# Subtracting the softmax maxima by accumulating DMAs in an encoder block on one core

## The chip, the core and the metric

The kernel runs on one core of a Trainium2 chip. The metric is device time in microseconds for one execution. Before the change three runs took 2291.91, 2293.18 and 2293.73 us; the median is 2293.18 us.

The core's engines run beside each other, each through its own queue of instructions, in order: TensorE (PE, with PEld for its weight loads), VectorE (DVE), ScalarE (ACT), GpSimd (POOL) and SyncE (SP). SP and POOL also issue DMAs; the 16 DMA engines carry them. Engines wait for one another by semaphores.

## The reference, cut to what matters

One layer of a bidirectional encoder on 2048 tokens plus 16 meta tokens: a projection, then grouped attention beside a Fourier mix, an output projection, and an MLP with squared ReLU. The change touches the softmax of attention:

```python
def attend(qb):
    s = jnp.einsum('bkgqd,bksd->bkgqs', qb, kt).astype(jnp.float32) * scale
    p = jax.nn.softmax(s, axis=-1).astype(vt.dtype)
    return jnp.einsum('bkgqs,bksd->bkgqd', p, vt)
```

There are 4 query heads and 2 key heads of 128 features, and all is computed in float32. The kernel splits an operand of a product into a high part and a low part (`hi`, `lo`) and multiplies three times (`mm3`, lines 80 to 82). The split is a cast on ScalarE (line 70) and a subtraction on VectorE (line 71).

## The kernel before

Attention is cut into 16 units, each of 256 tokens and one key head, that is 512 columns of queries (two heads). `attention()` is a generator; the Fourier mix, the output projections and the MLP pull steps of it between their own (`att.upto`), so that a unit lies interleaved with other matmuls. Attention runs from about 345 us, when the maxima of unit 0 are ready, to about 1560 us.

A unit's scores are laid out with keys on partitions and queries along the free axis. `scores(u, i)` makes tile i of 128 keys in one of two PSUM banks (tag `S`, two buffers), ScalarE copies it to SBUF (line 773), and two tiles make a *pair* `S` of 128 x 2 x 512 floats, 512 KB. There are eight pairs per unit, eight buffers for them, and a remainder of 96 rows for the meta tokens. A pair is called by its first tile in the rows below: `S_14_6` is the pair of tiles 6 and 7 of unit 14, the pair with j = 3. VectorE keeps a running maximum `M`.

`stats(u)` makes the maximum over all keys for each query, turns it and spreads it over all partitions; ScalarE copies the result from PSUM into `mb` (128 x 512, line 803). Then `softmax(u, i)` runs, i from 0 to 16. At an even i VectorE subtracts `mb` from a pair (line 832) and ScalarE takes the exponential (line 833), in place or, for the first pair, into the sum `acc`. At an odd i VectorE adds the pair to `acc` (line 839), the pair is split into `ph` and `pl`, and TensorE multiplies it with `v` into `o`. Meanwhile `scores(u + 1, i - 2)` fills the next unit's pairs into the buffers that come free. The first two units multiply unsplit (line 842).

The order on each engine is made by the framework's scheduler: it takes the instructions of the traced program by readiness in its own model of time and by their place in the program, and `issue_after` pins a few. So a change of what an instruction waits for can move rows on every engine.

POOL's queue holds the loads of attention (`q`, line 744; `kt`, line 711; `vt`, line 723), and small operations of the Fourier output (`ysq`, `rs_f`). SP's queue loads the MLP's weights (`wr_up`, `wr_dn`; three buffers of 256 KB).

## Time and profile before

| | |
|---|---|
| median of three runs | 2293.18 us |
| span of the profiled execution | 2291.4 us (the timed runs, without a profile, took 0.5 to 2.3 us more) |
| VectorE's subtractions of `mb` from pairs | 128, of 1.218 us each |
| bytes moved by DMA | 307.23 MB, mean 134 GB/s |
| of these through POOL's queue (q0, software) | 42.16 MB, 6.2% of 16 engines' span |

The page has the busy time of each engine, the costliest groups of instructions with their mean time and what ended the idle time before them, and the DMA queues. Other views are drawn from the same execution: busy time in chosen stretches, who waited for whom, and instructions in order of time. In a row of order of time the first number is the start, the second the time taken, and the bracket the idle time before it and what ended it.

The timed runs stand 0.5 to 2.3 us above the span of the profiled execution, which leaves out what lies around the program.

### The profile page before, as it was taken

To read this page: it belongs to the slowest core of one execution; us is meant where nothing else is said; L and a number is where in the kernel's file an instruction comes from. 1 tells how busy PE (TensorE), PEld (TensorE's weight loads), DVE (VectorE), ACT (ScalarE), POOL (GpSimd) and SP (SyncE) were. 2 spreads that over 40 slices of the span, in tenths; PEclk is the share of its full clock that TensorE was granted. 3 is DMA by queue.
4 is the path that set the end of the run, shared out by engine and by line. 5 is a ranking of instruction groups with operands and counts; after the bars stand their busy time and mean duration, and the time that the engine had idled before them with its cause. 6 is when DMAs were issued, how large, how long until landed. Compare 5 with 4: busy or idle time off the path is not lost.

```text
span 2291.4 us, 30005 instructions
## 1 busy us (share of the span) xinstructions
PE 2278.1 (99%) x10846; PEld 1883.0 (82%) x10846; DVE 1718.7 (75%) x2448; ACT 1280.6 (56%) x2303; POOL 184.0 (8%) x235
## 2 busy tenths in 40 slices
PE   9999999999999999999999999999999999999998
PEld 7888988777888888888888888888888888888887
DVE  6435588999986877986887877885875656697796
ACT  6443356566665655665765775664665545543344
POOL 2212120222000000000000100000000000200000
PEclk9999999999999999999999999999999999999999
DMA  6343252543533222333342453224454444865442
GB/s 213 100 119 102 78 169 79 190 137 120 166 117 108 96 87 79 114 114 106 97 157 87 157 175 104 92 82 170 140 177 158 152 152 156 303 193 165 129 138 83
DMA packets 178069, 307.23 MB, mean 134 GB/s; under 512 B 14960, under 2 KB 63728, under 8 KB 177536
## 3 DMA queue, kind: packets, MB, share of 16 engines
q1 hardware_dynamic: 159136, 262.89, 34.9%
q0 software_dynamic: 18640, 42.16, 6.2%
q8 instruction: 85, 1.39, 0.3%
q14 instruction: 64, 0.52, 0.1%
q10 hardware_dynamic: 144, 0.26, 0.0%
HBM read 225.27 MB, written 79.99 MB: 133 GB/s over the span
## 4 chain that ended last, share of the span: by engine, by line
PE 94%; DVE 3%; DMA 1%; ACT 1%; issue 1%; POOL 0%; SPq 0%; POOLq 0%; DVEq 0%; ACTq 0%
PE pdn L80 5%; PE pdn L82 5%; PE pdn L81 5%; PE pup L80 5%; PE pup L82 5%; PE pup L81 5%; PE s L80 3%; PE s L82 3%; PE s L81 3%; PE ux L80 2%; PE ux L81 2%; PE ux L82 2%; PE dx L80 2%; PE dx L82 2%; PE dx L81 2%; PE o L81 2%
## 5 line engine op out<-in xcount | busy, mean ns | idle before, releaser
L80 PE MATMUL pdn<-wh_dn,ah 128*128 128x512 f32 x512 | 201.5, 394 | 0.2 <-ACT r L1154 0.2
L80 PE MATMUL pup<-mTh,wh_up 128*128 128x512 f32 x512 | 201.5, 394 | 0.0
L81 PE MATMUL pup<-mTl,wh_up 128*128 128x512 f32 x512 | 200.7, 392 | 0.0
L82 PE MATMUL pup<-mTh,wl_up 128*128 128x512 f32 x512 | 200.4, 391 | 0.0
L81 PE MATMUL pdn<-wl_dn,ah 128*128 128x512 f32 x512 | 199.9, 390 | 0.0
L82 PE MATMUL pdn<-wh_dn,al 128*128 128x512 f32 x512 | 198.7, 391 | 0.0
L773 ACT COPY S<-s 128x512 f32<-128x512 f32 x256 | 148.4, 584 | 55.6 <-PE s L82 48.5
L70 ACT CAST wh_up<-wr_up 128x512 fp32r<-128x512 f32 x128 | 79.4, 620 | 164.3 <-PE pup L81 76.5
L832 DVE TENSOR_TENSOR S<-S,mb 128x1024 f32<-128x1024 f32 x128 | 154.8, 1218 | 8.4 <-ACT mb L803 8.2
L71 DVE TENSOR_TENSOR pl<-S,ph 128x512 fp32r<-128x512 f32 x196 | 132.3, 696 | 11.0 <-ACT ph L70 10.7
L833 ACT ACTIVATE S<-S 128x1024 f32<-128x1024 f32 x114 | 120.7, 1060 | 34.7 <-DVE S L832 34.1
L70 ACT CAST wh_dn<-wr_dn 128x512 fp32r<-128x512 f32 x128 | 79.1, 620 | 107.9 <-PE pdn L82 52.6
L71 DVE TENSOR_TENSOR wl_up<-wr_up,wh_up 128x512 fp32r<-128x512 f32 x128 | 87.6, 687 | 68.1 <-ACT wh_up L70 63.3
L839 DVE TENSOR_TENSOR acc<-acc,S 128x1024 f32<-128x1024 f32 x110 | 134.1, 1219 | 1.3 <-ACT S L833 1.1
L71 DVE TENSOR_TENSOR wl_dn<-wr_dn,wh_dn 128x512 fp32r<-128x512 f32 x128 | 87.2, 687 | 60.2 <-ACT wh_dn L70 51.8
L70 ACT CAST ph<-S 128x512 fp32r<-128x512 f32 x196 | 118.7, 620 | 15.9 <-PE o L82 12.5
L70 ACT CAST ah<-a 128x1024 fp32r<-128x1024 f32 x56 | 58.5, 1048 | 118.2 <-issue 60.8
L779 DVE TENSOR_TENSOR M<-M,S 128x1024 f32<-128x1024 f32 x96 | 118.0, 1229 | 6.7 <-ACT S L773 6.0
L80 PEld LDWEIGHTS pdn<-wh_dn,ah 128*128 128x128 f32 x512 | 96.1, 188 | 23.5 <-ACT r L1154 3.6
L80 PE MATMUL s<-q,kt 128*128 128x512 f32 (+1 forms) x272 | 113.0, 415 | 0.1
L82 PEld LDWEIGHTS pdn<-wh_dn,al 128*128 128x128 f32 x512 | 96.2, 188 | 19.9
L82 PEld LDWEIGHTS pup<-mTh,wl_up 128*128 128x128 f32 x512 | 96.2, 188 | 19.4
(345 smaller groups left out, 6413.0 us busy)
## 6 DMA issues: line engine op xcount, KB each, us to landing
wr_up<-in_w_up_dram SPq DMA_DIRECT2D x128, 256.0 KB, 2.8
wr_dn<-in_w_down_dram SPq DMA_DIRECT2D x128, 256.0 KB, 2.6
a<-s_d SPq DMA_DIRECT2D x42, 512.0 KB, 3.6
R<-in_w_up_dram SPq DMA_DIRECT2D x16, 1024.0 KB, 5.2
s_d<-s SPq DMA_DIRECT2D x64, 256.0 KB, 2.2
d<-in_w_down_dram SPq DMA_DIRECT2D x26, 512.0 KB, 5.0
s_d<-c SPq DMA_DIRECT2D x48, 256.0 KB, 2.4
x<-in_x_dram SPq DMA_DIRECT2D x16, 512.0 KB, 4.9
```

Source lines behind the costliest of these rows:

```text
L70: self.high = nc.scalar.copy(hi, src)
L71: self.low = nc.vector.tensor_tensor(lo, src, f32v(hi), op=ALU.subtract)
L80: nc.tensor.matmul(out, a[0], b[0], start=first, stop=False, skip_group_check=chain)
L81: nc.tensor.matmul(out, a[0], b[1], start=False, stop=False, skip_group_check=chain)
L82: nc.tensor.matmul(out, a[1], b[0], start=False, stop=last, skip_group_check=chain)
L773: nc.scalar.copy(S[:, i % 2], ps)
L779: nc.vector.tensor_tensor(M, M, S, op=ALU.max)
L832: nc.vector.tensor_tensor(S, S, mb, op=ALU.subtract)
L833: nc.scalar.activation(p, S, AF.Exp, scale=ISQ)
L839: nc.vector.tensor_tensor(acc, acc, p, op=ALU.add)
```

## The change

For the pairs 1 to 7 of each unit the subtraction is no longer an instruction of VectorE. ScalarE writes `mb` negated. Right after it `stats` traces an addition on VectorE for pair 0, and seven DMAs on POOL's queue which add the negated maxima, read twice for the two halves of a pair, to the pair in SBUF (`accum_op=ALU.add`). The remainder of 96 rows stays on VectorE, as an addition. The exponential of a pair now waits for its DMA.

```diff
@@ -800,7 +800,11 @@
             s = state[u]
             pd = rows_to_cols(over_keys(s["M"], f"m{u}", ALU.max), f"m{u}")
             mb = s["mb"] = ap2.tile([P, 512], F32, name=f"mb_{u}", tag="mb", bufs=1)
-            nc.scalar.copy(mb, pd)
+            nc.scalar.activation(mb, pd, AF.Copy, scale=-1.0)
+            both = mb.rearrange("p (o n) -> p o n", o=1).broadcast_to([P, 2, 512])
+            nc.vector.tensor_tensor(s["S"][0], s["S"][0], both, op=ALU.add)
+            for S in s["S"][1:-1]:
+                nc.gpsimd.dma_start(S, both, accum_op=ALU.add)
 
         def softmax(u, i):
 
@@ -809,7 +813,7 @@
             vt = s["v"]
             if i == NT:
                 S = s["S"][-1][:MR]
-                nc.vector.tensor_tensor(S, S, s["mb"][:MR], op=ALU.subtract)
+                nc.vector.tensor_tensor(S, S, s["mb"][:MR], op=ALU.add)
                 nc.scalar.activation(S, S, AF.Exp, scale=ISQ)
                 hi = ap2.tile([P, 512], R32, name="ph_" + nm, tag="ph", bufs=2)
                 acc = s["acc"]
@@ -828,8 +832,6 @@
             acc = s["acc"]
             p = acc if j == 0 and not s["native"] else S
             if i % 2 == 0:
-                mb = s["mb"].rearrange("p (o n) -> p o n", o=1).broadcast_to([P, 2, 512])
-                nc.vector.tensor_tensor(S, S, mb, op=ALU.subtract)
                 nc.scalar.activation(p, S, AF.Exp, scale=ISQ)
                 return
             v = vt[j // 2]
```

The first place is ScalarE's queue in unit 14, from the copy of the first score tile of unit 15 on. `S_14_k` are unit 14's pairs, `ph_14_5` the casts of the pair `S_14_4`, `s_15_k` score tiles of unit 15 in PSUM, and `wh_up` casts of MLP weights. Before:

```order
L773 COPY S_15_0_14039<-s_15_0_14035 128x512
L70 CAST wh_up_1_4_3_14181<-wr_up_1_4_3_14179 128x512
L70 CAST ph_14_5_0_14132<-S_14_4_13434 128x512
L70 CAST ph_14_5_1_14139<-S_14_4_13434 128x512
L773 COPY S_15_0_14039<-s_15_1_14074 128x512
L70 CAST wh_up_1_4_4_14220<-wr_up_1_4_4_14218 128x512
L833 ACTIVATE S_14_6_13499<-S_14_6_13499 128x1024
L773 COPY S_15_2_14111<-s_15_2_14107 128x512
L70 CAST wh_up_1_4_5_14246<-wr_up_1_4_5_14244 128x512
L833 ACTIVATE S_14_8_13590<-S_14_8_13590 128x1024
L70 CAST ph_14_7_0_14198<-S_14_6_13499 128x512
L773 COPY S_15_2_14111<-s_15_3_14146 128x512
```

And the changed kernel, from the same copy on:

```order
L773 COPY S_15_0_14045<-s_15_0_14041 128x512
L835 ACTIVATE S_14_8_13592<-S_14_8_13592 128x1024
L835 ACTIVATE S_14_10_13656<-S_14_10_13656 128x1024
L835 ACTIVATE S_14_12_13720<-S_14_12_13720 128x1024
L70 CAST ph_14_5_0_14137<-S_14_4_13438 128x512
L70 CAST ph_14_5_1_14144<-S_14_4_13438 128x512
L70 CAST wh_up_1_4_3_14185<-wr_up_1_4_3_14183 128x512
L773 COPY S_15_0_14045<-s_15_1_14080 128x512
L835 ACTIVATE S_14_14_13792<-S_14_14_13792 128x1024
L817 ACTIVATE S_14_16_13873<-S_14_16_13873 96x512
L70 CAST wh_up_1_4_4_14224<-wr_up_1_4_4_14222 128x512
L773 COPY S_15_2_14116<-s_15_2_14112 128x512
```

The exponentials have moved up: three of them now stand ahead of the casts of `S_14_4`, and the last pair's and the remainder's ahead of the copy of `s_15_2`, where before the exponential of `S_14_6` was the last to stand there.

The second place is POOL's queue from the load of unit 15's queries on. Before:

```order
L744 DMA q_15_13999<-q_d7_109 128x2x512
L192 TENSOR_TENSOR rs_a_15522<-ms_a_15520,mhalf_100 128x4
L1097 TENSOR_TENSOR rs_m_3_0_15722<-hsm_3_0_15616,mhalf_100 128x1
L1097 TENSOR_TENSOR rs_m_3_1_15726<-hsm_3_1_15621,mhalf_100 128x1
L1097 TENSOR_TENSOR rs_m_3_2_15730<-hsm_3_2_15626,mhalf_100 128x1
```

And the changed kernel:

```order
L744 DMA q_15_14006<-q_d7_109 128x2x512
L807 DMA S_14_2_13365<-mb_14_13924 128x2x512
L807 DMA S_14_4_13438<-mb_14_13924 128x2x512
L807 DMA S_14_6_13502<-mb_14_13924 128x2x512
L807 DMA S_14_8_13592<-mb_14_13924 128x2x512
L807 DMA S_14_10_13656<-mb_14_13924 128x2x512
L807 DMA S_14_12_13720<-mb_14_13924 128x2x512
L807 DMA S_14_14_13792<-mb_14_13924 128x2x512
L807 DMA S_15_2_14116<-mb_15_14657 128x2x512
```

Each unit's seven additions stand in a row, behind the load of the next unit's queries, and the next unit's seven behind them.

## The prediction

> **What bounds the kernel now.** I read the page's busy times first, then the one row for the stretch in which attention runs (345 to 1530 us), then who TensorE waits for in it.

> ```profile
> span 2291.4 us, 30005 instructions
> PE 2278.1 (99%) x10846; PEld 1883.0 (82%) x10846; DVE 1718.7 (75%) x2448; ACT 1280.6 (56%) x2303; POOL 184.0 (8%) x235
> ...
> 345.00:1530.00 1185.00, 1182.55 (x5453) 960.57 (x5452) 990.78 (x1373) 748.22 (x1296) 87.21 (x109) 1.00 0.37 118
> ...
> PE o L81 <- DVE pl L71: 0.8, 3, 0.4
> PE pmt L1126 <- ACT m L1121: 0.6, 1, 0.6
> PE pm_m L787 <- DVE M L768: 0.4, 1, 0.4
> ```

> The second row is time, then busy time of PE, PEld, DVE, ACT and POOL, the granted clock, the share of the 16 DMA engines, and GB/s. PE is busy 1182.55 of 1185.00 us at clock 1.00. VectorE is busy 990.78 of 1185.00, but what TensorE ever waits for in this stretch is 2.45 us in all, and only 1.2 us of that is put down to VectorE (0.8 for `pl`, 0.4 for `M`). So **whatever VectorE is relieved of, at most 2.45 us (0.1%) can be gained here**. The question is only whether the new way of subtracting makes PE wait.

> **The change part by part.** What goes and what carries on:

> ```profile
> L832 DVE TENSOR_TENSOR S<-S,mb 128x1024 f32<-128x1024 f32 x128 | 154.8, 1218 | 8.4 <-ACT mb L803 8.2
> L833 ACT ACTIVATE S<-S 128x1024 f32<-128x1024 f32 x114 | 120.7, 1060 | 34.7 <-DVE S L832 34.1
> L803 ACT COPY mb<-pd_m x16: 567/587/589, 344.9 to 1507.0; 128x512 f32<-128x512 f32 x16
> ```

> Removed: 112 of the 128 subtractions, 112 x 1.218 = 136 us of VectorE. By the waits above this is worth between 0 and 2.45 us; I take 0, because TensorE's work hides it. Pair 0 and the 96-row remainder stay on VectorE as additions of the same size, 0. The sign change rides on the copy of `mb` (0.587 us, 16 times); I take the same 0.59 us, and twice that would be 16 x 0.59 = 9 us of ACT, hidden under its 437 idle us of this stretch.

> Added: 7 DMAs of 512 KB in each of 16 units. The trace has no DMA that adds, and none from SBUF to SBUF. The nearest rows are POOL's plain loads of the same size, one of which (`kt`, at 355) ran almost alone:

> ```profile
> L711 POOL DMA_DIRECT2D kt<-k_d x20: 713/720/742, 314.0 to 1334.1; - x20
> ...
> q0 software_dynamic: 18640, 42.16, 6.2%
> ...
> q0 software_dynamic: 272, 0.52, 25.6%
> ...
> kt<-k_d POOLq DMA_DIRECT2D x1, 512.0 KB, 4.1
> ```

> The first 6.2% is of the whole span: 0.062 x 2291.4 = 142 us for 42.16 MB, so 1.77 us of all 16 engines for 0.524 MB; the window around the single `kt` gives 25.6% of 8 us, 2.05 us. It landed 4.1 us after its issue. An issue holds POOL 0.72 us: 7 x 0.72 = 5.0 us per unit, so POOL hands them out faster than they run. What the unit sees is a first landing L after `mb`, and then one landing every p; of the `kt`'s 4.1 us some 1.8 are its pass, so L = p + 2.3.

> - Lower end: the adding transfer costs a pass like a plain one, p = 1.8, L = 4.1.
> - Middle: to add, the destination is read besides the source, two reads for a write. Twice the page's figure is **p = 3.6**, L = 5.9.
> - Upper end: two reads, while the loads of other queues take some 0.28 of the engines (they are 0.37 busy in the row above, POOL's own loads among it): 3.6 / 0.72 = 5.0, L = 7.3.

> I take p = 3.6. The single `kt` had its engines nearly to itself, while the loads beside a unit's burst are not nothing, so the middle leans on neither.

> Now the place that pays. Before, an exponential stood in ACT's queue where VectorE had time for its subtraction (34.1 of the 34.7 us ahead of them are waits for it), and unit 14's eight ran from 1427.34 to 1457.72. In the changed order they are drawn together: the exponentials of `S_14_8`, `S_14_10` and `S_14_12` stand ahead of the casts of `S_14_4` (`ph_14_5_0`), and that of `S_14_14`, the seventh addition, ahead of the copy of `s_15_2`. **ACT works in order, so a late landing holds up rows that need no DMA.** When TensorE needs these rows, in unit 14:

> ```profile
> 1425.47 0.59 ACT L803 COPY mb<-pd_m 128x512 f32<-128x512 f32 x1 [1.40 <-PE pd_m L796]
> 1427.34 1.06 ACT L833 ACTIVATE acc<-S 128x1024 f32<-128x1024 f32 x1 [1.29 <-DVE S L832]
> ...
> 1442.89 0.62 ACT L70 CAST wh_up<-wr_up 128x512 fp32r<-128x512 f32 x1 [1.91 <-PE pup L81]
> ...
> 1444.38 0.57 ACT L773 COPY S<-s 128x512 f32<-128x512 f32 x1
> ...
> 1446.32 0.39 PE L80 MATMUL o<-ph,vt 128*128 128x512 f32 x1
> ...
> 1451.08 0.39 PE L80 MATMUL s<-q,kt 128*128 128x512 f32 x1
> ...
> 1457.72 1.07 ACT L833 ACTIVATE S<-S 128x1024 f32<-128x1024 f32 x1
> ...
> L813 ACT ACTIVATE S<-S x16: 612/627/633, 379.3 to 1547.6; 96x512 f32<-96x512 f32 x16
> ```

> `mb` is ready at 1426.06. TensorE takes up the third group of `o` at 1446.32. Ahead of it on ACT stand the exponential of the sixth DMA (1.06) and one cast (0.62 as `wh_up`'s), with an estimated 0.2 for the handing over: the sixth has to land by 1444.4, 18.4 us after `mb`. At 1451.08 TensorE starts `s_15_4`, which needs the PSUM bank of `s_15_2` (there are two), whose copy stands behind the seventh exponential: 1.06 + 0.63 (remainder) + 0.62 (`wh_up`) + 0.57 (copy) = 2.9, so the seventh has to land 22.1 us after `mb`. The DMAs land at L + 5p and L + 6p:

> - p = 1.8: 13.1 and 14.9 us. Nothing waits.
> - p = 3.6: 23.9 and 27.5 us, **5.4 us late**.
> - p = 5.0: 32.3 and 37.3 us, 15.2 us late.

> Where the seventh exponential used to stand, at 1457.72, 31.7 us after `mb`, p = 3.6 would have been in time: the new order sets the price as much as the DMA does.

> Within a unit the delays don't add, since TensorE's later needs shift with the first; across units they do, because TensorE has no idle time to take them up. I counted the seventh landing in all sixteen units from ACT's new order and the old times of `mb` (the first 344.9, the last 1507.0, in the row above): it is needed after 20 to 24 us in ten, after 15 to 17 in three (the first two and the last), after 30 to 33 in three. That averages 22.6, so unit 14 stands for the mean. **16 x 5.4 = 86 us.** At p = 5.0 it is 16 x 15.2 = 243 us, at p = 1.8 about 0.

> The rest I cost at nothing. Loads of weights meet fuller DMA engines, but the old kernel has such a stretch, where the engines were 0.91 busy and PE lost nothing:

> ```profile
> 1320.00:1341.00 21.00, 21.00 (x101) 16.75 (x100) 12.20 (x16) 12.73 (x25) 2.16 (x3) 1.00 0.91 295
> ```

> If that cover failed it would show as waits of ACT for `wr_up` and `wr_dn`. On POOL, the powers for `rs_f` (out_f, units 2 to 4) and the loads of `vt` now stand behind seven issues, 5.0 us; the powers are computed a row block ahead, which hides that, and without it three units would lose up to 3 x 5 = 15 us. The loads of `q` and `kt` stand ahead of the seven as before.

> Sum, against the profiled execution: 2291.4 + 0 + 86 = 2377.4 us of span. The median of the runs stands 1.8 us above that span, so **about 2380 us**, 3.8% slower.

> [...]

> **The rivals.**

> 1. *The queue keeps up, no change.* If an adding DMA moves at up to 2.3 us each (L = 4.6), the seventh lands within 18.4 us of `mb`, ahead of the 22.1. Only the first two units and the last would lose some 2 to 4 us each. Time 2291 to 2300. For it: the plain pass of 1.77 us; its price turns where 2.3 + 7p = 22.1, at p = 2.8. Against it: the destination must be read too. [...]
> 2. *Read, add and write one after the other.* If an addition takes its passes in series and shares the engines, p is 7.5 (three plain passes of 1.8, over 0.72), L = 9.8: the seventh lands 54.8 us after `mb`, 32.7 us late, 16 x 32.7 = 523 us, 2816 us. For it: nothing in this trace shows how an addition is pipelined. Against it: plain loads are.
> 3. *VectorE had been the bound after all, faster.* Its third figure in these rows is 95 to 97 of 100 us:

> ```profile
> 400.00:500.00 100.00, 98.74 (x453) 76.09 (x452) 96.69 (x137) 62.22 (x117) 26.98 (x32) 1.00 0.50 164
> 500.00:600.00 100.00, 99.76 (x458) 79.45 (x457) 95.33 (x138) 61.19 (x112) 20.28 (x26) 1.00 0.49 161
> ```

>    With 136 us less, TensorE's 2.45 us and perhaps as much inside rows that count as busy would go: 2288 us. Against it: the waits above.
> 4. *POOL can't hand the seven out at once* and is held until earlier ones have moved, so that `rs_f` and `vt` come late: the 15 us above on top of the forecast, 2395 us.

> **How the numbers follow.** Forecast (two reads, p between 2.8 and 5.0): 58%. Rival 1: 21%. Rival 2 (anything beyond p = 5.0): 13%. Rival 3: 4%. Rival 4: 4%. A measurement of this kernel can tell about 0.2% (4.6 us) from no change. Rival 1 falls half within 0.2% and half above it, and a small part of the forecast's low end comes out as no change: faster 4%, same 12%, slower 84%. The range goes from the lower bound's time, 2291, to p = 5.0, 2293 + 243 = 2536; some 4% lie below and 14% above.

> **What would show it.** Right: in the changed profile PE loses 60 to 150 us between 345 and the last unit, spread over all units; ACT's exponentials wait for DMA landings, and behind them TensorE waits for `ph`, for copies of `s` and for `wh`; the seven landings of a unit come 3 to 4.5 us apart; VectorE's busy time falls by about 136 us; q0 carries 59 MB more and its share rises by some 17% of the span. Wrong: landings under 2.5 us apart with PE at 1182 of 1185 (rival 1), over 5 us apart (rival 2), or PE waiting for `rs_f` or `wr_up` and not for what stands behind an exponential.

## The result and the profile after

The changed kernel takes **2451.64 us** (median of four runs, 2450.76 to 2453.22) against 2293.40 us for the kernel before, run beside it: a ratio of 1.0692, 95% interval 1.0677 to 1.0707. It is 6.9% slower. The forecast was 2380 us, 3.8% slower, with a range up to 2536. The sign and the range held; 72 us of the loss were missing from the sum.

The page of the changed kernel: busy time of the engines, the software DMA queue q0 with packets, MB and its share of 16 engines, and the costliest group that waits (count, then busy time and mean ns, then its idle time and what ended it).

```profile
span 2449.0 us, 30120 instructions
PE 2330.7 (95%) x10846; PEld 1902.4 (78%) x10846; DVE 1606.8 (66%) x2336; ACT 1278.6 (52%) x2303; POOL 319.9 (13%) x347
...
q0 software_dynamic: 49104, 100.89, 19.9%
...
L835 ACT ACTIVATE S<-S 128x1024 f32<-128x1024 f32 x114 | 120.4, 1058 | 170.8 <-DMA S<-mb 168.2
```

ScalarE's 34 us of waiting ahead of the exponentials have become 170.8, nearly all of it for the additions. VectorE is relieved of 112 us (1718.7 to 1606.8), and TensorE, with the same 10846 matmuls, is busy 52.6 us *longer*. That last figure was in no part of the forecast.

The windows view for the stretch in which attention runs in the changed kernel, the columns as in the prediction (time; busy PE, PEld, DVE, ACT, POOL; granted clock; DMA share; GB/s), and behind it the view of cores for the kernel before and for the changed one:

```profile
345.00:1690.00 1345.00, 1236.69 (x5463) 981.58 (x5462) 885.14 (x1269) 751.22 (x1304) 223.19 (x221) 0.96 0.58 148
```

```profile
core 0: 2291.4 us, clock 0.999
```

```profile
core 0: 2449.0 us, clock 0.979
```

The stretch held 5453 matmuls in 1185 us before and holds 5463 in 1345 us now. TensorE is idle in 1345.00 - 1236.69 = 108.3 us of it, where it was idle in 2.45: **105.9 us of waiting**. It is busy 1236.69 instead of 1182.55, **54.1 us longer**, at a mean clock of 0.96. Two different losses, about two to one.

Who TensorE waits for in that stretch (in total, times, longest):

```profile
PE o L80 <- ACT ph L70: 29.9, 9, 7.2
PE s L80 <- ACT S L773: 13.2, 6, 7.7
PE pup L80 <- DVE h L1182: 13.0, 5, 3.5
PE o L81 <- DVE pl L71: 12.7, 11, 5.5
PE pdn L80 <- DVE h L1182: 8.6, 3, 3.7
PE poa L80 <- DMA at<-o_d: 6.3, 1, 6.3
PE pa L570 <- DVE alo L576: 4.9, 1, 4.9
```

The casts `ph` and the copies of `s` behind late exponentials were forecast; with the 2.8 us that the unsplit units wait for exponentials themselves they make 45.9 of the 105.9 us, and 58.6 with `pl`, which VectorE makes from `ph`. `h` (the MLP's rows, 25 us with its smaller rows), `at` (the attention output read back, 10.6 us) and `alo` (the Fourier part) were not.

Unit 14, the unit that carried the prediction: GpSimd's issues of the seven additions in order of time. Its `mb` starts at 1563.30 and is ready at 1563.90.

```profile
1564.32 3.73 POOL L807 DMA_DIRECT2D S<-mb  x3 [7.45 <-ACT mb L803]
1569.89 1.19 POOL L807 DMA_DIRECT2D S<-mb  x1 [1.84 <-DVE pl L71]
1573.76 1.22 POOL L807 DMA_DIRECT2D S<-mb  x1 [2.68 <-DVE acc L841]
1577.40 1.20 POOL L807 DMA_DIRECT2D S<-mb  x1 [2.42 <-DVE pl L71]
1580.85 1.19 POOL L807 DMA_DIRECT2D S<-mb  x1 [2.24 <-DVE h L1182]
```

Three go out at once; the fourth to the seventh only 3.4 to 3.9 us apart, although GpSimd has nothing else to do. The packets of the trace say why: the additions land at 1569.22, 1573.06, 1576.70, 1580.12, 1583.54, 1587.27 and 1592.07, and each issue from the fourth on comes 0.7 us behind the next landing. The releasers in the brackets are VectorE rows that happened to end then; the landing is what fits every row. So the first addition lands 5.3 us after `mb`, the seventh 28.2 us after it, one every 3.8 us (5.9, 27.5 and 3.6 had been forecast). Over all units the medians are 5.3 and 26.6 us, 3.6 us apart.

What the stall in this unit does to the clock, in the windows view of the changed kernel, columns as above:

```profile
1577.00:1585.40 8.40, 7.52 (x33) 5.83 (x32) 4.86 (x7) 4.18 (x5) 2.39 (x2) 1.00 1.10 205
1585.40:1589.30 3.90, 0.43 (x3) 0.01 (x1) 0.03 (x1) 1.63 (x3) 0.00 (x0) 1.00 1.09 255
1589.30:1590.60 1.30, 1.07 (x4) 0.66 (x4) 1.30 (x3) 1.30 (x3) 0.00 (x0) 0.99 1.03 326
1590.60:1594.00 3.40, 3.40 (x10) 2.62 (x8) 2.92 (x3) 1.69 (x4) 0.00 (x0) 0.50 0.79 276
1594.00:1600.00 6.00, 6.00 (x27) 4.69 (x25) 5.37 (x7) 4.41 (x10) 0.00 (x0) 1.00 0.24 76
```

TensorE is idle for 3.5 us up to 1589.3. It resumes at full clock, and then for 3.4 us the clock is 0.50: the matmuls take 0.63 us instead of 0.39 and start 0.43 us apart instead of 0.23. This stall of 3.5 us so cost another 1.7. In the whole of attention the trace's record of the granted clock has 16 such stretches, of 3.41, 6.83 or 10.24 us, 99.0 us in all. Eight of them begin while TensorE still stands, and in 23.9 of the 99.0 us it does nothing that half speed could slow; the other 75.1 us cost it 37.5 us. Of the 54.1 us that it is busy longer, another 2.2 are the ten matmuls more that the stretch holds; of the remaining 14 us some 12 are counted at full clock: there a matmul right behind idle time adds 0.50 us to the busy time in the mean, any other 0.22, and there are 51 such (14.6 us more than at 0.22), where the kernel before has 11 at 0.43 (2.3 us more). The view of cores gives (1 - 0.979) x 2449.0 = 51 us against 2 us before: this counts all time at half clock, idle time too.

### The profile page after: what moved, and what is told of

Read it like the earlier page. It is cut to its first block, busy times and chain, and to the rows that moved or that the text cites. A ratio compares the mean times of both kernels' runs of the same rounds, so it can differ in the third digit from the quotient of the medians.

```text
span 2449.0 us, 30120 instructions
## 1 busy us (share of the span) xinstructions
PE 2330.7 (95%) x10846; PEld 1902.4 (78%) x10846; DVE 1606.8 (66%) x2336; ACT 1278.6 (52%) x2303; POOL 319.9 (13%) x347
## 3 DMA queue, kind: packets, MB, share of 16 engines
q0 software_dynamic: 49104, 100.89, 19.9%
## 5 line engine op out<-in xcount | busy, mean ns | idle before, releaser
L80 PE MATMUL pup<-mTh,wh_up 128*128 128x512 f32 x512 | 205.8, 402 | 13.0 <-DVE h L1182 13.0
L80 PE MATMUL pdn<-wh_dn,ah 128*128 128x512 f32 x512 | 204.2, 399 | 10.3 <-DVE h L1182 8.6
L835 ACT ACTIVATE S<-S 128x1024 f32<-128x1024 f32 x114 | 120.4, 1058 | 170.8 <-DMA S<-mb 168.2
L81 PE MATMUL pup<-mTl,wh_up 128*128 128x512 f32 x512 | 203.9, 398 | 0.0
L81 PE MATMUL pdn<-wl_dn,ah 128*128 128x512 f32 x512 | 201.7, 394 | 0.0
L71 DVE TENSOR_TENSOR pl<-S,ph 128x512 fp32r<-128x512 f32 x196 | 134.0, 700 | 72.6 <-ACT ph L70 69.1
L807 POOL DMA_DIRECT2D S<-mb x112 | 135.8, 1420 | 300.1 <-ACT mb L803 160.0
L773 ACT COPY S<-s 128x512 f32<-128x512 f32 x256 | 148.1, 582 | 48.2 <-PE s L82 43.2
L70 ACT CAST wh_up<-wr_up 128x512 fp32r<-128x512 f32 x128 | 79.2, 619 | 173.1 <-PE pup L81 101.8
L71 DVE TENSOR_TENSOR wl_up<-wr_up,wh_up 128x512 fp32r<-128x512 f32 x128 | 87.9, 688 | 116.2 <-ACT wh_up L70 111.5
L71 DVE TENSOR_TENSOR wl_dn<-wr_dn,wh_dn 128x512 fp32r<-128x512 f32 x128 | 87.3, 688 | 90.4 <-ACT wh_dn L70 81.9
L70 ACT CAST wh_dn<-wr_dn 128x512 fp32r<-128x512 f32 x128 | 79.0, 618 | 121.7 <-PE pdn L82 57.8
L779 DVE TENSOR_TENSOR M<-M,S 128x1024 f32<-128x1024 f32 x96 | 117.8, 1227 | 21.1 <-ACT S L773 20.3
L80 PE MATMUL s<-q,kt 128*128 128x512 f32 (+1 forms) x272 | 115.8, 426 | 13.2 <-ACT S L773 13.2
L70 ACT CAST ph<-S 128x512 fp32r<-128x512 f32 x196 | 117.4, 617 | 16.7 <-PE o L82 14.2
L80 PEld LDWEIGHTS pup<-mTh,wh_up 128*128 128x128 f32 x512 | 98.2, 192 | 35.7 <-DVE h L1182 15.4
L80 PEld LDWEIGHTS pdn<-wh_dn,ah 128*128 128x128 f32 x512 | 97.2, 190 | 36.1 <-DVE h L1182 5.8
L70 ACT CAST ah<-a 128x1024 fp32r<-128x1024 f32 x56 | 58.5, 1048 | 118.8 <-issue 61.1
L80 PE MATMUL o<-ph,vt 128*128 128x512 f32 x224 | 91.9, 410 | 29.9 <-ACT ph L70 29.9
## 6 DMA issues: line engine op xcount, KB each, us to landing
S<-mb POOLq DMA_DIRECT2D x112, 512.0 KB, 10.2
a<-s_d SPq DMA_DIRECT2D x42, 512.0 KB, 3.7
d<-in_w_down_dram SPq DMA_DIRECT2D x26, 512.0 KB, 5.0
```

The costliest lines, as they stand in the source:

```text
L70: self.high = nc.scalar.copy(hi, src)
L71: self.low = nc.vector.tensor_tensor(lo, src, f32v(hi), op=ALU.subtract)
L80: nc.tensor.matmul(out, a[0], b[0], start=first, stop=False, skip_group_check=chain)
L81: nc.tensor.matmul(out, a[0], b[1], start=False, stop=False, skip_group_check=chain)
L773: nc.scalar.copy(S[:, i % 2], ps)
L779: nc.vector.tensor_tensor(M, M, S, op=ALU.max)
```

## The experiments

"Idle" and "busy" are TensorE's in the stretch from 345 us to the same matmul as above (5449 to 5470 of them). The last column is (1 - clock) x span, idle time at half clock included.

| kernel | us | ratio, 95% interval | idle | busy | clock loss |
|---|---|---|---|---|---|
| before | 2293.4 | 1 | 2.5 | 1182.6 | 2 |
| changed | 2451.6 | 1.0692 (1.0677 to 1.0707) | 108.3 | 1236.7 | 51 |
| e1_plain | 2304.1 | 1.0048 (1.0032 to 1.0064) | 8.0 | 1188.0 | 9 |
| e10_plain_halves | 2302.6 | 1.0048 (1.0031 to 1.0065) | 5.0 | 1184.0 | 2 |
| e3_vector | 2322.3 | 1.0131 (1.0111 to 1.0151) | 19.3 | 1195.7 | 9 |
| e7_vector_hold | 2322.6 | 1.0131 (1.0116 to 1.0146) | 20.3 | 1194.7 | 7 |
| e2_hold | 2401.0 | 1.0480 (1.0462 to 1.0497) | 75.7 | 1217.3 | 36 |
| e4_hold_split | 2378.9 | 1.0379 (1.0363 to 1.0394) | 56.4 | 1212.6 | 31 |
| e5_no_weights | 2335.8 | 1.0191 (1.0175 to 1.0206) | 30.4 | 1196.6 | 16 |
| e11_only_weights | 2420.0 | 1.0554 (1.0538 to 1.0569) | 83.2 | 1228.8 | 43 |
| e6_three_out | 2369.1 | 1.0334 (1.0318 to 1.0349) | 51.6 | 1209.4 | 28 |
| e9_close | 2312.2 | 1.0084 (1.0069 to 1.0099) | 14.4 | 1190.6 | 7 |
| e8_four | 2309.3 | 1.0073 (1.0056 to 1.0090) | 13.2 | 1187.8 | 2 |
| e12_three | 2293.1 | 1.0001 (0.9992 to 1.0010) | 4.0 | 1182.0 | 0 |

### The pace of the additions: e1_plain and e10_plain_halves

```diff
-                nc.gpsimd.dma_start(S, both, accum_op=ALU.add)
+                nc.gpsimd.dma_start(S, both)
```

> Leaves out the addition: the seven DMAs of a unit write the negated maxima over the pairs, with the same bytes written, the same queue and the same order of issue as the changed kernel. Theory (the destination has to be read as well, so an adding transfer costs two passes): landings of a unit about 2.0 us apart where the changed kernel has 3.8, the seventh some 17 us after mb, before it is needed; time 2293 to 2310 us, TensorE idle under 15 us between 345 us and the last unit. Rival (it is POOL's queue that sets the pace, by issuing late or holding few transfers, whatever they do): landings stay 3 us or more apart, and the time stays above 2400 us.

The seven transfers without the addition are all there 13.7 us after `mb` in the median, 1.7 us apart, and the time is 2304.1 us, as the theory had it. The issues, in the view of line 807, first of the changed kernel, then of this one (ns min/median/max):

```profile
L807 POOL DMA_DIRECT2D S<-mb x112: 1178/1210/2255, 346.0 to 1670.9; - x112
...
DMA to landing us min/median/max: 5.2/10.2/13.5
```

```profile
L807 POOL DMA_DIRECT2D S<-mb x112: 722/724/763, 346.2 to 1523.8; - x112
...
DMA to landing us min/median/max: 3.2/6.4/11.6
```

Plain, all seven go out one behind the other at 0.72 us; adding, an issue takes 1.21 us and only three are out at a time. The queue's share gives the work on the engines: (0.199 x 2449.0 - 142)/112 = 3.08 us of all 16 for an addition, (0.132 x 2302.4 - 142)/112 = 1.45 us for a plain transfer, 142 us being q0's load in the kernel before. The addition more than doubles it. But in the trace's packets an addition also moves in 256 pieces of 2 KB, the plain transfer in 128 of 4 KB; the next kernel splits the plain one in two, to give it such pieces.

```diff
-                nc.gpsimd.dma_start(S, both)
+                for e in range(2):
+                    nc.gpsimd.dma_start(S[:, e], mb)
```

> As e1_plain (DMAs that write the negated maxima and add nothing), but each pair in two DMAs of 128x512, 256 KB each, so that a partition's piece is 2 KB, as in the additions, and not 4 KB, as in e1_plain. What slows an addition to 3.8 us a pair: if the reading of the destination, a pair takes 1.7 to 2.4 us here and the time is 2295 to 2315; if the smaller pieces, a pair takes 3 us or more and the time is above 2340.

A pair takes 1.9 us (in unit 5 the fourteen landings lie between 3.3 and 15.8 us after `mb`), 1.48 us of all engines by q0's share of 13.4% of 2297.6 us, and the time is that of e1. But the edit did not do what it was for: in the trace's packets the halves too move in pieces of 4 KB, 64 to a half, so this run says nothing on the size of pieces. Something on it can be read from the kernel before, whose plain loads of `q` and `vt` on the same queue do move 512 KB in 256 pieces of 2 KB: all q0 packets of 2 KB there take 120 ns in the mean, so an estimated 256 x 0.120 / 16 = 1.9 us of all engines for 512 KB, where the additions' pieces of the same size take 191 ns, 3.06 us. If pieces within SBUF cost what these loads from DRAM cost, their size is some 0.5 of the 1.6 us by which an addition is dearer, and the adding is the rest; whether that rest is a second read, as the forecast took it, no run here shows.

### The new place without any DMA: e3_vector and e7_vector_hold

```diff
-                nc.gpsimd.dma_start(S, both, accum_op=ALU.add)
+                nc.vector.tensor_tensor(S, S, both, op=ALU.add)
```

> The changed kernel with all eight additions of a unit on VectorE, at the place where the changed kernel traces them, and no DMA among them. Theory: sign and place of the addition cost nothing, 2290 to 2297 us. Rival (what is lost comes with the new place, by which the scheduler draws the exponentials together): 2310 us or more.

> No additions by DMA: all eight on VectorE in the change's new place, as in e3_vector (2322.3 us), and besides the exponentials held behind the casts of the pair before. If e3's 29 us come from the exponentials that moved ahead of rows which TensorE needs, they go: 2292 to 2300. If they come from VectorE, whose eight additions (8 x 1.22 us in one piece) now stand ahead of pl and h, they stay: 2316 to 2326.

The place alone, which I had taken for harmless, costs 30 us: 2322.3 us, and 2322.6 us with the exponentials held. So of the two readings of e7_vector_hold the second holds, and the 30 us come from VectorE. Unit 6 of e7_vector_hold, VectorE's rows in order of time, and TensorE's row behind them:

```profile
749.52 1.23 DVE L805 TENSOR_TENSOR S<-S,mb 128x1024 f32<-128x1024 f32 x1
750.66 8.03 DVE L807 TENSOR_TENSOR S<-S,mb 128x1024 f32<-128x1024 f32 x7
758.61 0.68 DVE L789 TENSOR_REDUCE mx_l<-pm_l 128x4 f32<-128x512 f32 x1
759.21 0.74 DVE L1184 SCALAR_TENSOR_TENSOR h<-pdn,sc,h 128x512 f32<-128x512 f32 x1
```

```profile
760.01 0.50 PE L80 MATMUL pup<-mTh,wh_up 128*128 128x512 f32 x1 [3.16 <-DVE h L1184]
```

Eight additions in one piece hold VectorE for 9.2 us, the MLP's `h` stands behind them, and TensorE waits 3.16 us for it. Before the change the same work was dealt out between other rows and cost nothing. This is not part of the changed kernel's loss, since there only one of the eight is left on VectorE; it shows that the moment at which the subtractions are made has a price of its own, whoever makes them.

### The exponentials put back: e2_hold and e4_hold_split

```diff
             if i % 2 == 0:
-                nc.scalar.activation(p, S, AF.Exp, scale=ISQ)
+                with tc.issue_after(s["ph"]) if "ph" in s else nullcontext():
+                    nc.scalar.activation(p, S, AF.Exp, scale=ISQ)
...
                 split(hi, lo, p[:, e])
+                s["ph"] = ins_of(split.high)
```

> The changed kernel with one edit: in units 2 to 15 the exponential of a pair is issued on ACT behind the casts of the pair before it, so that no late landing holds up casts and copies that don't need it. The DMAs are the same. Theory (ACT's order around the exponentials turns the landings into stalls): landings stay 3.8 us apart, but TensorE's loss in units 2 to 15 goes; units 0 and 1, which have no casts and keep their order, keep their 13 us each; 2310 to 2330 us, granted clock back at 1.00 in units 2 to 15. Rival (the fuller DMA engines and the occupied POOL delay weights and powers, whatever the order): most of the 158 us stays, 2400 us or more.

Holding each exponential behind the casts of the pair before gives 50.7 us back, not the 120 to 140 that the theory asked for. In e4_hold_split the first two units, which the hold does not reach, also add on VectorE, and 98 additions stay with the DMAs:

```diff
             for S in s["S"][1:-1]:
-                nc.gpsimd.dma_start(S, both, accum_op=ALU.add)
+                if s["native"]:
+                    nc.vector.tensor_tensor(S, S, both, op=ALU.add)
+                else:
+                    nc.gpsimd.dma_start(S, both, accum_op=ALU.add)
```

> The edit of the run with held exponentials, and units 0 and 1 add on VectorE; units 2 to 15 still add their seven pairs by DMA, 98 DMAs in all. Theory: nothing is left that makes TensorE wait, so the old time: 2288 to 2298 us, with VectorE relieved of 98 x 1.22 = 120 us, which buys at most the 2.45 us that TensorE waited before. Rival (the fuller DMA engines and the occupied POOL cost time of their own): 2310 us or more.

Another 22.0 us, in units 0 and 1, and the theory has failed: 86 us of loss are still there, although ScalarE's wait for additions has fallen from 168.2 to 29.8 us. What it waits for now, in e4_hold_split:

```profile
ACT wh_up L70 <- DMA wr_up<-in_w_up_dram: 59.4, 11, 17.4
...
ACT wh_oa L73 <- DMA wr_oa<-in_w_out_dram: 35.9, 9, 13.6
...
ACT S L839 <- DMA S<-mb: 29.8, 18, 3.7
...
ACT wh_dn L70 <- DMA wr_dn<-in_w_down_dram: 23.8, 8, 10.4
```

119 us of waiting for **weights**, where the kernel before has 15 (6.7 for `wr_up`, 4.8 for `wr_oa`, 3.5 for `wr_dn`). The longest one, SP's queue and then ScalarE's row:

```profile
774.51 1.79 SPq L871 DMA_DIRECT2D o_d<-ohl  x2
783.07 5.18 SPq L1059 DMA_DIRECT2D at<-o_d  x3
788.35 2.85 SPq L986 DMA_DIRECT2D wr_up<-in_w_up_dram  x2
```

```profile
795.89 0.62 ACT L70 CAST wh_up<-wr_up 128x512 fp32r<-128x512 f32 x1 [17.37 <-DMA wr_up<-in_w_up_dram]
```

And the same 30 us by stretch, additions issued from 767.66 on:

```profile
766.00:776.00 10.00, 10.00 (x51) 8.12 (x51) 8.40 (x13) 6.29 (x11) 4.95 (x4) 1.00 0.80 148
776.00:786.00 10.00, 10.00 (x46) 8.29 (x45) 5.43 (x9) 2.52 (x5) 3.62 (x3) 1.00 1.10 209
786.00:796.00 10.00, 1.87 (x9) 1.21 (x7) 0.00 (x0) 0.11 (x1) 0.00 (x0) 0.74 1.04 267
796.00:806.00 10.00, 8.90 (x30) 6.89 (x31) 8.65 (x11) 8.70 (x15) 0.00 (x0) 0.74 0.29 86
```

The DMA share stands above 1 for 20 us. The store of `o` goes out at 774.5 into the middle of it. From issue to landing the stores and read-backs take, in the median, in the kernel before and then in the changed one (in e4_hold_split 9.4 and 8.0 us):

```profile
o_d<-ohl SPq DMA_DIRECT2D x32, 256.0 KB, 2.5
at<-o_d SPq DMA_DIRECT2D x32, 256.0 KB, 4.3
```

```profile
o_d<-ohl SPq DMA_DIRECT2D x32, 256.0 KB, 9.3
at<-o_d SPq DMA_DIRECT2D x32, 256.0 KB, 7.9
```

SP issues these in the order of its queue: the read-back `at` waits for that store until 783, and the weights that are queued behind `at` go out at 788 and land at 795. TensorE stands still for 8 of 10 us, and the clock is halved on both sides of 796.

### The late weights: e5_no_weights and e11_only_weights

```diff
-        raw = wp.tile([P, 512], F32, name="wr_" + name, tag="wr", bufs=3)
-        nc.sync.dma_start(raw, src)
+        if len(RAW) < 3:
+            RAW.append(wp.tile([P, 512], F32, name="wr_" + name, tag="wr", bufs=3))
+            nc.sync.dma_start(RAW[-1], src)
+        raw = RAW[len(USED) % len(RAW)]
+        USED.append(raw)
```

> The kernel of e4_hold_split (exponentials held in their old place, units 0 and 1 on VectorE, 98 adding DMAs), with one more thing left out: of the 288 loads of wr_up, wr_dn and wr_oa in the MLP and the output projection only the first three are made, and their tiles are used again (so these weights are wrong). Theory, late weights: in e4 ScalarE waits 59.4 + 35.9 + 23.8 = 119 us for weights whose loads meet full DMA engines (share 1.0 to 1.1 while the seven additions run), and TensorE behind it. Without these loads units 5 to 15 lose next to nothing and what is left is units 2 to 4, some 21 us: 2300 to 2330 us. Rival, the weights are late only because something else has already held TensorE (a held POOL, the store and load of o): within 15 us of e4's 2379.

2335.8 us: 43.1 us back, half of what was left, 6 us outside the expected range. From one unit's `mb` to the next, the three intervals from unit 2 to unit 5 still lose 6.4, 5.8 and 7.6 us (19.8, as expected), and the interval from 8 to 9 loses 10.8. TensorE's waits for `at` in all of attention are these, and 7.7 of the 11.2 us lie in that interval:

```profile
PE poa L82 <- DMA at<-o_d: 5.9, 3, 3.1
PE poa L80 <- DMA at<-o_d: 5.3, 1, 5.3
```

The same edit on the changed kernel itself, with nothing held:

> The changed kernel, nothing held, with only three of the 288 weight loads made, as in e5_no_weights (weights wrong by it). There it gave 43 us back. Theory, two chains beside each other: in the changed kernel the exponentials' wait for the additions comes first and hides the late weights (ScalarE waits 168 us for additions, 8 us for weights), so little is won: 2425 to 2452. Rival, late weights cost here what they cost there: 2400 to 2415.

2420.0 us, below the range of the one theory and above that of the rival: 31.7 us back. So the weights' loads cost the changed kernel too, although ScalarE waited only 18 us for weights there (15 before) while it waited 168 for additions. The wait that a view names is the one that ended last, not the only one that was late. One caution holds for both kernels: without the weights' 75 MB the engines have more room (a DMA share of 0.45 in attention in both, where e4_hold_split and the changed kernel have 0.58), and the additions land a little earlier as well (the seventh 25.5 us after `mb` in the median, against 26.6). How much of the 32 to 43 us comes from weights being late, and how much from this room, is not separated.

### GpSimd held, and all causes at once: e6_three_out and e9_close

```diff
+                elif j < 4:
                     nc.gpsimd.dma_start(S, both, accum_op=ALU.add)
...
+                    exp = nc.scalar.activation(p, S, AF.Exp, scale=ISQ)
+                if not s["native"] and 1 <= j <= 4:
+                    with tc.issue_after(ins_of(exp)):
+                        nc.gpsimd.dma_start(s["S"][j + 3], s["both"], accum_op=ALU.add)
```

> The kernel of e4_hold_split, but only the additions of pairs 1 to 3 are issued when mb is ready; those of pairs 4 to 7 are each issued behind the exponential of the pair three before, so that never more than three are out and GpSimd is not held in an issue. Theory, GpSimd held: rs_f is in time again, units 2 to 4 get back 15 to 25 us, the rest stays: 2354 to 2365. Rival, the full engines: spread over the softmax, one addition every 4 to 5 us leaves room for SP's loads, and units 5 to 15 gain too: 2300 to 2345. Other rival: the later issues make the last additions late and ScalarE waits for them: above 2379.

2369.1 us, 9.9 us better than e4_hold_split, less than the 15 to 25 expected. It is where it was expected: the intervals after units 2 and 3 lose 2.2 and 2.0 us instead of 6.0 and 6.2, the others as before. Spreading the issues leaves the engines as full as they were (a DMA share of 0.59 in attention against 0.58, the seventh landing 26.8 us after `mb`).

e9_close takes this together with e5's edit and reads `at` from another tensor, so that it waits for no store:

> The adding DMAs stay as they are in e4_hold_split (98 of them), but what has been named as the way their cost reaches TensorE is taken away all at once: exponentials held, units 0 and 1 on VectorE, never more than three additions out (as in e6_three_out), only three of the 288 weight loads made (as in e5_no_weights), and the loads of the attention output (at) read from the keys in DRAM instead, so that they wait for no store (weights and attention output are wrong by it). If these are all, little is left: 2292 to 2312. If the additions cost in a way not named yet: above 2320.

2312.2 us, the upper end. All 98 additions still run, and 67 of e4's 86 us are gone. Of the 20 us that stay, 10.1 lie between units 4 and 5, where a load of `at` is late even without the store ahead of it (TensorE waits 5.4 us for it).

### Fewer additions: e8_four and e12_three

```diff
-            for S in s["S"][1:-1]:
-                if s["native"]:
-                    nc.vector.tensor_tensor(S, S, both, op=ALU.add)
-                else:
+            for S in s["S"][4:-1]:
+                if not s["native"]:
                     nc.gpsimd.dma_start(S, both, accum_op=ALU.add)
...
             if i % 2 == 0:
+                if s["native"] and j or 1 <= j < 4:
+                    nc.vector.tensor_tensor(S, S, s["both"], op=ALU.add)
```

> The kernel of e4_hold_split with only the pairs 4 to 7 of a unit added by DMA (56 DMAs in 14 units instead of 98), pairs 1 to 3 on VectorE just ahead of their exponentials as before the change. The burst lasts some 16 us instead of 28. Theory, late weights: the three weight tiles cover a load for some 10 us, so only the part of the burst beyond that costs: 2300 to 2325. Rival, a cost in proportion to the number of additions: 2293 + 86 x 4/7 = 2342. Rival, the adds cost nothing once they are in time: 2293 to 2298.

> As e8_four, with only the pairs 5 to 7 of units 2 to 15 added by DMA (42 DMAs), so that all three are out at once, GpSimd is not held, and the burst is over some 13 us after the maxima. By the theory that only what outlasts the weight tiles' cover and what holds GpSimd costs, nothing is left of e8's 17 us but a few: 2292 to 2300. If the cost goes with the number of additions, three quarters of e8's 17 us stay: 2303 to 2308. In no theory is it faster than before by more than 0.2%: TensorE has 2.45 us to gain.

Four additions a unit (the last lands 16.5 us after `mb` in the median) cost 17 us; e12_three, the same with pairs 5 to 7 alone (the last after 12.5 us), costs nothing: 2293.1 us, ratio 1.0001. In steps from seven to four to three the loss is 86, 17 and 0 us, far from proportional. In e12_three the stores still take 7.0 us in the median and ScalarE waits 46.6 us for weights, and TensorE loses nothing by it: what is late has cover, that is, TensorE has other work in hand for as long. By the packets, of the 40 us behind a unit's first issue the DMA share is 0.95 or more for 26.5 us in e4_hold_split, 17 in e8_four and 12.5 in e12_three (medians). The plain transfers of e1_plain, all seven of a unit with nothing held, keep it there for 14.5 us and cost 12 us, so they fit in between. The additions left out in e8_four and e12_three are also those whose pairs are needed first, which these two runs alone do not separate from the length of the burst. The row of e12_three for attention:

```profile
345.00:1531.00 1186.00, 1181.97 (x5458) 961.61 (x5457) 948.38 (x1333) 745.65 (x1297) 147.88 (x151) 1.00 0.48 137
```

TensorE is back at 1182 of 1186 us and clock 1.00, with VectorE 42 us less busy than before. No version tried is faster than the kernel before.

## Why the prediction was right, and where it fell short

**Nothing to gain: right.** (Of TensorE's 2.45 us before, 1.6 were VectorE's and not 1.2: two waits of 0.2 us, for `ahi` and `ph`, were left out. That changes nothing.) e12_three takes 42 additions from VectorE and changes the time by 0.01%. VectorE's relief itself was put at 136 us and is 112; a subtraction's 1.22 us overlap its neighbours' (seven in a row took 8.03 us above), which is a part of it.

**The pace of the additions: right, in part by luck.** 3.6 us were taken; the median over the units is 3.6 and unit 14 has 3.8. The seventh landing was put at 27.5 us and came at 26.6 (28.2 in unit 14). But 3.6 was meant as an addition's own work on the engines, with nothing for the loads beside it. Its own work is 3.08 us, and with other transfers on the same engines one lands every 3.6: two misses that cancel. q0's share rose from 6.2 to 19.9% of the span, not by 17 points. That an addition costs two passes was the author's estimate. The runs show the ratio, 3.08 us of the engines against 1.45 to 1.48 plain, though the plain ones moved in larger pieces; a second read as such they do not show.

**The 5.4 us of unit 14 and their sum: the mechanism right, the size by luck.** Exponentials wait for landings, and TensorE behind them for `ph` and `s`, all along attention. In unit 14 TensorE is idle 5.35 us in all, the figure of the forecast, but not for the reason that gave it. The seventh addition landed 28.2 us after `mb`, later than the 27.5 taken, and held TensorE nowhere; the sixth did, through `ph`, for 3.47 us, and the rest are short waits for VectorE's `pl` and `h`. Over all units 86 us of waiting were forecast from this and 105.9 were measured, of which 46 to 59 are put down to rows behind exponentials; putting the exponentials back gave 50.7 us.

**"The new order sets the price as much as the DMA does": too much said.** With the exponentials back in place (e2_hold) a third of the loss goes, and the first two units hold another 22 us. What the DMAs do to other transfers is the larger rest. Because these waits run beside each other, no shares are fixed: without the weights' loads the changed kernel wins 31.7 us, the held one 43.1.

**"The rest I cost at nothing": the step that failed.** The buffers of the weights were to hide fuller engines, on the evidence of a row of 21 us with a DMA share of 0.91. That row held no addition, and no store of `o` with its read-back. With the additions in flight a store takes 9.3 us instead of 2.5, the read-back waits for it, and the weights stand behind the read-back in SP's queue (in e4_hold_split the three went out at 774.5, 783.1 and 788.4); ScalarE then waits up to 17.4 us for the weights. The prediction's own warning, ScalarE waiting for weights, is small in the changed kernel (18 us with `wr_oa`, 15 before) and shows in full (119 us) once the exponentials are out of the way. The 86 us that e4_hold_split still loses are the size of what was put at nothing; 67 of them went when the weights' loads, the store ahead of `at` and the hold on GpSimd were taken away together (e9_close).

**A term that was not in the sum: the clock.** Some 37.5 us, about half of the 72 us that were missing. Another 20 are waiting, 105.9 us instead of 86. Of the 15 stalls of TensorE over 3 us in attention, 14 met a stretch of 3.41, 6.83 or 10.24 us at half speed; one of 3.17 us, at 1335.8, did not, and two stretches followed stalls of 1.7 and 2.1 us. Shorter stalls met such a stretch in some cases only: of the nine between 1.6 and 2.7 us in the changed kernel these two did, two fell into a stretch that had begun, and five met none; the four of e3_vector are 2.5 to 2.7 us long and each is followed by 3.41 us at 0.5. In the kernel before, whose longest wait in attention is 0.6 us, the clock is 1.00 throughout attention. Had this been priced at one to two stretches of 3.41 us for each unit, an estimate from the lengths in this trace, 16 x 1.7 to 16 x 3.4 = 27 to 54 us would have been added to the forecast.

**The rivals.** The queue that keeps up is e1_plain, not the addition. Passes in series (7.5 us) did not appear. VectorE was not the bound. GpSimd is held, as the fourth rival had it (three additions out, then one issue per landing, some 17 us a unit): the powers `rs_f` come late by it, and being computed a row block ahead doesn't hide that. VectorE's `xo` never waited for them before, waits 13.9 us in the changed kernel and 16.5 in e4_hold_split, and 3.7 us in e6_three_out, where the hold is gone. That is worth 9.9 us there, against the 15 that were put on it.

**What stays open.** Whether an addition reads its destination in a pass of its own, and how the adding and the size of the pieces share the slower pace; how the weights' share and the additions' own divide, since taking one away speeds up the other; and what holds the last 20 us of e9_close outside units 4 and 5.

## What to carry to other kernels

Work moved to DMA engines is not free because the issuing side is: multiply its time on all 16 engines by its count in a burst, and compare the time for which the share then stands at 1 with what each other transfer in flight, stores and read-backs included, has as cover. Here a burst that kept the engines full for 12.5 us cost nothing, and the loss then grew much faster than the number of additions (three, four, seven: 0, 17, 86 us). And here, with TensorE as the bound, a stall had to be priced with the half speed that came with 14 of the 15 over 3 us: 1.7 us on top for one of 3.5 us in unit 14, and over all of attention 37.5 us on top of 105.9 us of waiting.
